# A two-layer token mixer in float32: the weight pairs of one chunk per MLP layer in another order

## The chip, the core and the metric

The kernel runs on one core of a Trainium2 chip. The metric is the device time of one execution in microseconds (us); the median of three runs of the kernel before is 2252.37 us (2251.97 to 2252.53). The engines are TensorE (PE, matrix products into the accumulator memory PSUM), VectorE (DVE) and ScalarE (ACT, both elementwise), GpSimd (POOL) and SyncE (SP, which here issues the loads). Each works through its own queue in order and waits at semaphores for the others.

## The reference

256 tokens of width 2048 go through two layers, in float32. Each layer is a mixer with an input and an output projection, and an MLP of hidden width 8192:

```python
for l in range(DEPTH):                                   # DEPTH = 2
    u = rmsnorm(h, g[0])
    ...                                                  # mixer: y
    h = h + rmsnorm(y, g[1])
    u = rmsnorm(h, g[2])
    z = jnp.square(jax.nn.relu(u @ mlp_w1[l])) @ mlp_w2[l]
    h = h + rmsnorm(z, g[3])
```

The change touches the product `u @ mlp_w1[l]` alone.

## The kernel before

**Split products.** Every float32 operand is split into a high part (a cast by ACT) and a residual (operand minus high part, by DVE). A product of two tiles is three matmuls into one accumulator: high x high, high x residual of the weight, residual of the activation x high. Lines 236 to 238 are these three in an ordinary block, lines 360 to 362 in the summed pairs described below.

**Tiling.** The 256 tokens are two row tiles (t = 0, 1) of 128. The width 2048 is sixteen k-tiles of 128. A load (L220, or L327 in the pairs) brings a slab: two k-tiles by 512 columns of a weight matrix, 512 KB, into one of seven `raw` tiles. ACT casts it to `whi` (L223, L331) and DVE forms `wlo` (L224, L332) in one of six pairs of tiles (`W_BUFS`). A slab of an ordinary block takes 12 matmuls.

**The MLP.** The hidden width is worked through in eight chunks of 1024 columns. For chunk c, `up(c)` computes the hidden values and `down(c)` multiplies them by 1024 rows of W2; the order is up(0), up(1), down(0), up(2), down(1) and so on. up(0) is two ordinary blocks of 512 columns. up(1) to up(7) are done by the class `Pairs`: eight pairs of k-tiles (k-tiles 2p and 2p + 1), each by the full 1024 columns, that is two slabs L (left 512 columns) and R. The string `PAIRS = "SSCSSCSC"` says how each pair is done.

- A **C** pair is ordinary: eight products of (row tile, column half, k-tile), 24 matmuls; two slabs, each cast once, two of the six tile pairs.
- An **S** pair is a 2 x 2 by 2 x 2 block product with seven products in place of eight, 21 matmuls. It needs sums of weight tiles and sums of activation tiles. The weight sums are four additions on DVE (L336), which overwrite the raw tiles; the pair then has `plain` (L as it is), `r1` (half of R), `two` (two sums) and `four` (two more sums), and takes four of the six tile pairs. The products are called p1, p2, q3, q5, p7, p6, q4; p1 and p2 use `plain`, q3 `r1`, q5 and p7 `two`, p6 and q4 `four`. The sums of activation tiles (class `Differences`, L294, L301, L304, L305) are made once per layer for the pairs 0, 1, 3, 4 and 6, during up(0).

Some products are shared by several outputs. After the last S pair (`end`), a copy on ACT (L392) and four additions on DVE (L373) combine them; the last C pair then finishes each output tile with another addition (L373) and the squared ReLU (L596). These are the twelve closing operations of DVE. The four output tiles are transposed by PE (L175, four matmuls each), split again (L162, L163), and are operands of down(1), one phase later. The hidden tiles of up(0) pass the same steps (L584, L586, L175, L162, L163) during the first pairs of up(1), and their transposes use the accumulators `acc` (three buffers), as do the products p1, p2 and bR; the other products use `aux` (five buffers).

**What sets the order.** `run` walks the slabs or pairs in order: load, then matmuls, then what is due (`later`, L422). A scheduler then orders each engine's queue ahead of the run; it may move a matmul or an addition past others that do not depend on it. On the chip the queues are fixed.

Of the kernel before, what the change touches and what calls it, by code (L numbers as in the profile page):

```python
# [22 lines left out]
NT = 2  # L23
# [2 lines left out]
W_BUFS = 6  # L26
LEAD = 6
PAIRS = "SSCSSCSC"
ACC_BUFS = 3
AUX_BUFS = 5  # L30
TAIL = 4
# [8 lines left out]
def trunk(ctx, tc, x, x_t, norm_g, ng_cols, e_win, rbf, e_wout, o_win, lbraw, smalls, wa2, ba, o_wout, w1, w2,  # L40
          c_ident, c_flip, c_mask, out):
    nc = tc.nc
# [7 lines left out]
    dram = ctx.enter_context(tc.tile_pool(name="dram", bufs=1, space=bass.MemoryType.DRAM))  # L50
    accp = ctx.enter_context(tc.tile_pool(name="accp", bufs=ACC_BUFS, space=PSUM))
    auxp = ctx.enter_context(tc.tile_pool(name="auxp", bufs=AUX_BUFS, space=PSUM))

    def aux():
        return auxp.tile([P, 512], F32, name="aux")
# [116 lines left out]
    def transpose4(src, pool=auxp, name="aux"):  # L172
        ps = pool.tile([P, 512], F32, name=name)
        for k in range(4):
            nc.tensor.transpose(out=ps[:, k * P:(k + 1) * P], in_=src[:, k * P:(k + 1) * P], identity=ident)  # L175
        return ps

    class XT:
        def __init__(self):
            self.g = {}  # L180
# [21 lines left out]
    def w_pair():  # L202
        return [wp.tile([P, SLAB, 512], F32R, name="w" + n) for n in ("hi", "lo")]

    class Block:
# [7 lines left out]
        def load(self, s):  # L213
            k0 = self.kts[s * SLAB]
            raw = rawp.tile([P, SLAB, 512], F32, name="raw")
            hi, lo = w_pair()
            n = slice(0, self.n)
            fine = s in self.fine
            for a, b in ((0, 1), (1, 2)) if fine else ((0, SLAB),):
                nc.sync.dma_start(out=raw[:, a:b, n], in_=self.wv[:, k0 + a:k0 + b, self.n0:self.n0 + self.n])  # L220
                if fine:
                    self.beside[a]()
                nc.scalar.copy(out=hi[:, a:b, n], in_=raw[:, a:b, n])  # L223
                nc.vector.tensor_tensor(out=lo[:, a:b, n], in0=raw[:, a:b, n], in1=hi[:, a:b, n], op=ALU.subtract)  # L224
            self.w[s] = (hi, lo)
# [84 lines left out]
    class Pairs:  # L310
# [6 lines left out]

        nslab = len(PAIRS)

        def __init__(self, wv, n0, X, diffs, U, evac):  # L320
            self.wv, self.n0, self.X, self.diffs, self.U, self.evac = wv, n0, X, diffs, U, evac
            self.w, self.ps = {}, {}

        def load(self, s):
            raws = [rawp.tile([P, SLAB, 512], F32, name="raw") for _ in range(2)]
            for raw, n in zip(raws, (self.n0, self.n0 + 512)):
                nc.sync.dma_start(out=raw, in_=self.wv[:, 2 * s:2 * s + 2, n:n + 512])  # L327

            def conv(raw, i=slice(0, SLAB)):
                hi, lo = w_pair()  # L330
                nc.scalar.copy(out=hi[:, i, :], in_=raw[:, i, :])  # L331
                nc.vector.tensor_tensor(out=lo[:, i, :], in0=raw[:, i, :], in1=hi[:, i, :], op=ALU.subtract)  # L332
                return hi, lo

            def add(dst, a, b):
                nc.vector.tensor_tensor(out=dst, in0=a, in1=b, op=ALU.add)  # L336

            L, R = raws
            if PAIRS[s] == "C":
                self.w[s] = [conv(L), conv(R)]  # L340
                return
            plain = conv(L)
            r1 = conv(R, slice(1, 2))
            add(R[:, 1, :], R[:, 1, :], R[:, 0, :])
            add(R[:, 0, :], R[:, 0, :], L[:, 0, :])
            two = conv(R)
            add(L[:, 0, :], L[:, 0, :], R[:, 1, :])
            add(L[:, 1, :], L[:, 1, :], L[:, 0, :])
            self.w[s] = [plain, r1, two, conv(L)]

        def product(self, n, s, x, w, i):
            first = n not in self.ps
            if first:
                self.ps[n] = accp.tile([P, 512], F32, name="acc") if n in ("bR", "p2", "p1") else aux()
            ps, (xh, xl), (hi, lo) = self.ps[n], x, w
            if n in ("q5", "p7", "p6", "p1"):
                stop = "S" not in PAIRS[s + 1:]
            else:
                stop = s == self.nslab - 1 and i == SLAB - 1
            nc.tensor.matmul(ps, xh, hi[:, i, :], start=first, stop=False)  # L360
            nc.tensor.matmul(ps, xh, lo[:, i, :], start=False, stop=False)  # L361
            nc.tensor.matmul(ps, xl, hi[:, i, :], start=False, stop=stop)  # L362

        def mm(self, s, t):
            if t == 0:
                return
            x = [[self.X.get(t, 2 * s + i) for i in range(2)] for t in range(NT)]
            w = self.w.pop(s)
            z = self.ps
            s1, u, u3 = self.U  # L370

            def add(n, a, b, op=ALU.add):
                nc.vector.tensor_tensor(out=n, in0=a, in1=b, op=op)  # L373

            if PAIRS[s] == "C":
                for n, t, j in (("p2", 0, 0), ("q3", 0, 1), ("q4", 1, 0), ("bR", 1, 1)):
                    for i in range(2):
                        self.product(n, s, x[t][i], w[j], i)
                    if s == self.nslab - 1:
                        o = self.out[t, j]  # L380
                        if j == 0:
                            add(o, z[n], s1 if t == 0 else u3)
                        else:
                            add(o, z[n], o)
                        self.evac(t, j, o)
                return
            d = self.diffs[s]
            L, r1, two, four = w
            end = "S" not in PAIRS[s + 1:]
            self.product("p1", s, x[0][0], L, 0)  # L390
            if end:
                nc.scalar.copy(out=s1, in_=z["p1"])  # L392
            self.product("p2", s, x[0][1], L, 1)
            self.product("q3", s, d.get(3), r1, 1)
            self.product("q5", s, d.get(0), two, 0)
            self.product("p7", s, d.get(2), two, 1)
            self.product("p6", s, d.get(1), four, 0)
            if end:
                self.out = {(t, j): self.evac.tile() for t in range(NT) for j in range(2)}
                add(u, z["p6"], s1)  # L400
                add(u3, z["p7"], u)
                add(self.out[0, 1], z["q5"], u, ALU.subtract)
                add(self.out[1, 1], z["q5"], u3, ALU.subtract)
            self.product("q4", s, x[1][1], four, 1)
# [17 lines left out]
    def later(f, slabs=2):  # L422

        soon.append([slabs, f])
# [50 lines left out]
    def wview(w):  # L475
        return w.rearrange("(kt p) n -> p kt n", p=P)
# [87 lines left out]
    def mlp(l, X, rst, factors, y, ypool, spool, mid, between, lead):  # L564
        diffs, U, late = {}, [], {}
        hid = {}
        w1v, w2v = wview(w1[l]), wview(w2[l])
# [12 lines left out]
        def up(c):  # L580
            def mk(j):
                def evac(t, ps):
                    r = ypool.tile([P, 512], F32, name="relu", bufs=2)
                    nc.scalar.activation(out=r, in_=ps, func=AF.Relu)  # L584
                    r2 = ypool.tile([P, 512], F32, name="ulo", bufs=4)
                    nc.vector.tensor_tensor(out=r2, in0=r, in1=r, op=ALU.mult)  # L586
                    later(lambda: hid[c].put(t, c * 2 + j, split4(x2p, "x2", transpose4(r2, accp, "acc"))))
                return evac

            hid[c] = Hid()  # L590
            if c == 0:
                return [Block(w1v, j * 512, 512, ALLK, X.get, mk(j)) for j in range(2)]
            n = [0]

            def evac(t, j, z):
                nc.vector.scalar_tensor_tensor(out=z, in0=z, scalar=0.0, in1=z, op0=ALU.max, op1=ALU.mult)  # L596
                n[0] += 1
                later(lambda: hid[c].put(t, c * 2 + j, split4(x2p, "x2", transpose4(z))), 2 + 2 * n[0])
            evac.tile = lambda: ypool.tile([P, 512], F32, name="ulo", bufs=4)
            return [Pairs(w1v, c * 1024, X, diffs, U, evac)]  # L600

        def down(c):
            def mk(nb):
# [19 lines left out]
        def difference(p):  # L623
            diffs[p] = Differences(spool, X, p)
            diffs[p].make(lambda: ypool.tile([P, 512], F32, name="relu", bufs=2))
# [5 lines left out]

        work = [lambda p=p: difference(p) for p in range(len(PAIRS)) if PAIRS[p] == "S"]
        hooks = {LEAD + 1 + 2 * i: [f] for i, f in enumerate(work)}
# [19 lines left out]
    X = XIn()  # L653
# [560 lines left out]
```

## Time and profile before

The table is taken from one profiled execution.

| | before |
|---|---|
| time of the profiled execution | 2252.14 us |
| its span, first to last instruction | 2250.3 us |
| median of three runs | 2252.37 us |
| mean granted TensorE clock | 0.999 |
| ACT busy | 1162.1 us (52%) |
| bytes moved | 440.87 MB, mean 196 GB/s |

The profile's timeline gives the start of an instruction, its duration, engine, line, operation, output and inputs, and in brackets how long the engine was idle before it and what ended that. A duration runs to the result's arrival: the next instruction of the same engine often starts before it. up(1) of layer 0 runs on PE from 431.97 to 474.93 us after the span's start; that of layer 1 is the same 1161.6 us later.

### The profile page before, as it was taken

How to read it: one execution, taken by the hardware profiler on the slowest of the kernel's cores; microseconds unless marked ns; L12 is line 12 of the kernel's file. 1: busy time of each engine (PE TensorE's matmuls, PEld its weight loads, DVE VectorE, ACT ScalarE, POOL GpSimd, SP SyncE). 2: the span in 40 equal slices, each digit the busy share in tenths (PEclk: the TensorE clock that was granted, in tenths of full speed). 3: DMA queues.
4: the chain of work that ended last, by engine and by line, in shares of the span. 5: the costliest groups of instructions: out<-in, count | busy, mean ns of one | idle time of the engine just before them, and what ended most of it. 6: DMA issues, size and time to landing. Idle time of an engine off the chain costs nothing.

```text
span 2250.3 us, 28788 instructions
## 1 busy us (share of the span) xinstructions
PE 2230.9 (99%) x10556; PEld 1849.3 (82%) x10556; DVE 1746.8 (78%) x2328; ACT 1162.1 (52%) x1598; POOL 20.6 (1%) x40
## 2 busy tenths in 40 slices
PE   9999999999999999999999999999999999999998
PEld 7888888888888888888788888888788888888886
DVE  6656656988898898896867767657979889889876
ACT  7444445655455455454746454546555445445443
POOL 0000000000000000000100000000000000000000
PEclk9999999999999999999999999999999999999999
DMA  9565576575565575586655545576556566566673
GB/s 348 167 181 169 169 265 187 175 231 171 187 230 167 187 237 158 197 288 192 212 174 166 152 150 156 170 241 201 156 196 233 160 206 218 169 207 202 198 262 101
DMA packets 222560, 440.87 MB, mean 196 GB/s; under 512 B 13745, under 2 KB 14545, under 8 KB 222417
## 3 DMA queue, kind: packets, MB, share of 16 engines
q1 hardware_dynamic: 218880, 429.18, 59.2%
q0 software_dynamic: 2816, 8.99, 1.1%
q8 instruction: 83, 1.36, 0.2%
q10 hardware_dynamic: 720, 0.85, 0.1%
q14 instruction: 61, 0.49, 0.1%
HBM read 430.57 MB, written 8.40 MB: 195 GB/s over the span
## 4 chain that ended last, share of the span: by engine, by line
PE 90%; DVE 6%; ACT 1%; issue 1%; DMA 1%; DVEq 0%; ACTq 0%; SPq 0%
PE acc L236 18%; PE acc L238 18%; PE acc L237 18%; PE aux L361 4%; PE aux L362 4%; PE aux L360 4%; PE acc L275 3%; PE aux L275 3%; PE acc L362 3%; PE acc L361 3%; PE acc L360 3%; PE aux L175 2%; DVE raw L336 2%; DVE wlo L332 2%; PE aux L272 2%; PE acc L272 2%
## 5 line engine op out<-in xcount | busy, mean ns | idle before, releaser
L224 DVE TENSOR_TENSOR wlo<-raw,whi 128x1024 fp32r<-128x1024 f32 (+1 forms) x561 | 676.2, 1220 | 343.4 <-ACT whi L223 341.5
L223 ACT CAST whi<-raw 128x1024 fp32r<-128x1024 f32 (+1 forms) x561 | 585.6, 1054 | 635.4 <-PE acc L238 486.1
L236 PE MATMUL acc<-whi,x 128*128 128x512 f32 x1280 | 502.9, 393 | 0.0
L331 ACT CAST whi<-raw 128x1024 fp32r<-128x1024 f32 x364 | 337.5, 968 | 319.4 <-DVE raw L336 214.0
L238 PE MATMUL acc<-whi,x 128*128 128x512 f32 x1280 | 498.9, 390 | 0.0
L237 PE MATMUL acc<-wlo,x 128*128 128x512 f32 x1280 | 498.7, 390 | 0.0
L332 DVE TENSOR_TENSOR wlo<-raw,whi 128x1024 fp32r<-128x1024 f32 x364 | 394.2, 1118 | 59.6 <-ACT whi L331 56.0
L238 PEld LDWEIGHTS acc<-whi,x 128*128 128x128 f32 x1280 | 240.3, 188 | 50.6
L237 PEld LDWEIGHTS acc<-wlo,x 128*128 128x128 f32 x1280 | 240.5, 188 | 48.5
L236 PEld LDWEIGHTS acc<-whi,x 128*128 128x128 f32 x1280 | 240.4, 188 | 48.4
L236 PE MATMUL acc<-whi,xt 128*128 128x512 f32 x640 | 253.5, 398 | 0.8 <-ACT xt L672 0.7
L237 PE MATMUL acc<-wlo,xt 128*128 128x512 f32 x640 | 250.8, 392 | 3.3 <-DVE wlo L224 2.1
L238 PE MATMUL acc<-whi,xt 128*128 128x512 f32 x640 | 250.5, 392 | 0.0
L336 DVE TENSOR_TENSOR raw<-raw 128x512 f32<-128x512 f32 x280 | 193.8, 692 | 9.3
L237 PEld LDWEIGHTS acc<-wlo,xt 128*128 128x128 f32 x640 | 120.3, 188 | 29.7 <-DVE wlo L224 6.3
L238 PEld LDWEIGHTS acc<-whi,xt 128*128 128x128 f32 x640 | 120.1, 188 | 25.9 <-DVE xt L168 0.6
L236 PEld LDWEIGHTS acc<-whi,xt 128*128 128x128 f32 x640 | 119.9, 188 | 25.9 <-ACT xt L672 1.6
L360 PE MATMUL acc<-whi,xt 128*128 128x512 f32 x308 | 120.1, 390 | 0.0
L362 PE MATMUL acc<-whi,xt 128*128 128x512 f32 x308 | 119.9, 389 | 0.0
L361 PE MATMUL acc<-wlo,xt 128*128 128x512 f32 x308 | 119.9, 389 | 0.0
L360 PE MATMUL aux<-whi,s 128*128 128x512 f32 x280 | 109.4, 392 | 2.3 <-ACT whi L331 2.3
L361 PE MATMUL aux<-wlo,s 128*128 128x512 f32 x280 | 110.5, 395 | 1.0 <-DVE wlo L332 1.0
(228 smaller groups left out, 2541.9 us busy)
## 6 DMA issues: line engine op xcount, KB each, us to landing
raw<-w SPq DMA_DIRECT2D x512, 512.0 KB, 4.9
raw<-o_win SPq DMA_DIRECT2D x112, 512.0 KB, 3.8
raw<-e_win SPq DMA_DIRECT2D x95, 512.0 KB, 3.9
raw<-e_wout SPq DMA_DIRECT2D x32, 512.0 KB, 4.1
raw<-o_wout SPq DMA_DIRECT2D x32, 512.0 KB, 4.0
s<-norm_g SPq DMA_DIRECT2D x8, 512.0 KB, 6.3
mid<-s POOLq DMA_DIRECT2D x8, 512.0 KB, 3.9
s<-mid SPq DMA_DIRECT2D x8, 512.0 KB, 7.1
```

The costliest lines, as they stand in the source:

```text
L223: nc.scalar.copy(out=hi[:, a:b, n], in_=raw[:, a:b, n])
L224: nc.vector.tensor_tensor(out=lo[:, a:b, n], in0=raw[:, a:b, n], in1=hi[:, a:b, n], op=ALU.subtract)
L236: nc.tensor.matmul(ps, xh, hi[:, i, 0:self.n], start=first, stop=False)
L237: nc.tensor.matmul(ps, xh, lo[:, i, 0:self.n], start=False, stop=False)
L238: nc.tensor.matmul(ps, xl, hi[:, i, 0:self.n], start=False, stop=last)
L275: nc.tensor.matmul(self.ps[j], hi[:, i, cs], x, start=s == 0 and i == 0, stop=False)
L331: nc.scalar.copy(out=hi[:, i, :], in_=raw[:, i, :])
L332: nc.vector.tensor_tensor(out=lo[:, i, :], in0=raw[:, i, :], in1=hi[:, i, :], op=ALU.subtract)
L336: nc.vector.tensor_tensor(out=dst, in0=a, in1=b, op=ALU.add)
L360: nc.tensor.matmul(ps, xh, hi[:, i, :], start=first, stop=False)
L361: nc.tensor.matmul(ps, xh, lo[:, i, :], start=False, stop=False)
L362: nc.tensor.matmul(ps, xl, hi[:, i, :], start=False, stop=stop)
```

## The change

For c = 1 alone, in both layers, the eight pairs are taken in the order START: pair 2 (a C), 0, 1, 5 (a C), 3, 4, 6, 7 (a C). The kinds in the order of work are C S S C S S S C, where they were S S C S S C S C. The other six chunks go through `range(8)` as before.

```diff
+START = (2, 0, 1, 5, 3, 4, 6, 7)
...
-        def __init__(self, wv, n0, X, diffs, U, evac):
+        def __init__(self, wv, n0, X, diffs, U, evac, seq):
...
+            self.seq = seq
+            self.kinds = "".join(PAIRS[p] for p in seq)
...
-                nc.sync.dma_start(out=raw, in_=self.wv[:, 2 * s:2 * s + 2, n:n + 512])
+                nc.sync.dma_start(out=raw, in_=self.wv[:, 2 * self.seq[s]:2 * self.seq[s] + 2, n:n + 512])
...
-            if PAIRS[s] == "C":
+            if self.kinds[s] == "C":
...
-                stop = "S" not in PAIRS[s + 1:]
+                stop = "S" not in self.kinds[s + 1:]
...
-            x = [[self.X.get(t, 2 * s + i) for i in range(2)] for t in range(NT)]
+            x = [[self.X.get(t, 2 * self.seq[s] + i) for i in range(2)] for t in range(NT)]
...
-            d = self.diffs[s]
+            d = self.diffs[self.seq[s]]
-            end = "S" not in PAIRS[s + 1:]
+            end = "S" not in self.kinds[s + 1:]
...
-            return [Pairs(w1v, c * 1024, X, diffs, U, evac)]
+            return [Pairs(w1v, c * 1024, X, diffs, U, evac, START if c == 1 else range(len(PAIRS)))]
```

Lines behind the new constant move down by one, lines behind the constructor by three: L332 becomes L335, L336 becomes L339, L373 becomes L376, L596 becomes L599, L586 becomes L589, L224 becomes L225, L236 to L238 become L237 to L239, L175 becomes L176. The number of instructions of each kind is the same. Three places of the queues follow, in layer 0; layer 1 is alike.

First, VectorE's queue at the first pairs. `wlo<-raw,whi` of 128x1024 is a residual of a whole slab, of 128x512 that of `r1`; `raw<-raw` are the additions of an S pair; `relu` and `s<-relu` belong to the activation sums, `ulo<-relu` to the hidden tiles of up(0). Before, from the third addition of the first S pair on:

```order
L336 TENSOR_TENSOR raw<-raw 128x512
L301 TENSOR_TENSOR relu<-relu 128x128
L336 TENSOR_TENSOR raw<-raw 128x512
L305 TENSOR_TENSOR s<-relu,s 128x512
L332 TENSOR_TENSOR wlo<-raw,whi 128x1024
L586 TENSOR_TENSOR ulo<-relu 128x512
L332 TENSOR_TENSOR wlo<-raw,whi 128x1024
L586 TENSOR_TENSOR ulo<-relu 128x512
L332 TENSOR_TENSOR wlo<-raw,whi 128x512
L336 TENSOR_TENSOR raw<-raw 128x512 x4
L332 TENSOR_TENSOR wlo<-raw,whi 128x1024
```

Of the change, from the residual of `two` of the first S pair (now the second pair) on, to the residuals behind the second S pair's additions:

```order
L335 TENSOR_TENSOR wlo<-raw,whi 128x1024
L589 TENSOR_TENSOR ulo<-relu 128x512 x2
L339 TENSOR_TENSOR raw<-raw 128x512
L335 TENSOR_TENSOR wlo<-raw,whi 128x1024 x2
L335 TENSOR_TENSOR wlo<-raw,whi 128x512
L164 TENSOR_TENSOR x_4028<-acc,x_4028 128x512
L339 TENSOR_TENSOR raw<-raw 128x512 x3
L164 TENSOR_TENSOR x_4036<-acc,x_4036 128x512
L335 TENSOR_TENSOR wlo<-raw,whi 128x1024
L339 TENSOR_TENSOR raw<-raw 128x512
L335 TENSOR_TENSOR wlo<-raw,whi 128x1024 x4
```

The fourth addition of an S pair stood ahead of another operation or among four in a row; in the first two S pairs it now stands alone, directly ahead of the residual of `four`, which is formed from the tile that it writes.

Second, VectorE's queue at the end of up(1), from the fourth additions of the last S pair on. `s<-aux`, `ulo<-aux` and `ulo<-acc` are the combinations, `ulo<-ulo` the squared ReLU. Before:

```order
L336 TENSOR_TENSOR raw<-raw 128x512 x4
L332 TENSOR_TENSOR wlo<-raw,whi 128x1024 x4
L373 TENSOR_TENSOR s<-aux,s 128x512
L224 TENSOR_TENSOR wlo<-raw,whi 128x1024
L373 TENSOR_TENSOR s<-aux,s 128x512
L373 TENSOR_TENSOR ulo<-aux,s 128x512 x2
L373 TENSOR_TENSOR ulo<-acc,s 128x512
L373 TENSOR_TENSOR ulo<-aux,ulo 128x512
L596 SCALAR_TENSOR_TENSOR ulo<-ulo 128x512 x2
L373 TENSOR_TENSOR ulo<-aux,s 128x512
L373 TENSOR_TENSOR ulo<-acc,ulo 128x512
L596 SCALAR_TENSOR_TENSOR ulo<-ulo 128x512 x2
```

Of the change:

```order
L335 TENSOR_TENSOR wlo<-raw,whi 128x1024 x3
L376 TENSOR_TENSOR s<-aux,s 128x512
L335 TENSOR_TENSOR wlo<-raw,whi 128x1024
L376 TENSOR_TENSOR s<-aux,s 128x512
L376 TENSOR_TENSOR ulo<-aux,s 128x512 x2
L376 TENSOR_TENSOR ulo<-acc,s 128x512
L376 TENSOR_TENSOR ulo<-aux,ulo 128x512
L599 SCALAR_TENSOR_TENSOR ulo<-ulo 128x512 x2
L376 TENSOR_TENSOR ulo<-aux,s 128x512
L376 TENSOR_TENSOR ulo<-acc,ulo 128x512
L599 SCALAR_TENSOR_TENSOR ulo<-ulo 128x512 x2
L225 TENSOR_TENSOR wlo<-raw,whi 128x1024 x3
```

The first residual of the next block (L224, now L225) stood second among the closing operations; now it stands behind all of them, and the residual of the last C pair's right slab has its place. On ScalarE the copy L392 stood directly ahead of the last C pair's casts; it now stands ahead of four casts, those of the last S pair's `two` and `four` and the last C pair's.

Third, TensorE's queue at the seam between up(1) and down(0), where `acc<-whi,x` and `acc<-wlo,x` are down(0)'s matmuls and `aux<-ident,ulo` the transposes of up(1)'s hidden tiles. Before, twelve matmuls of down(0) stand ahead of these rows (the last two of them shown), and two more transposes stand 93 matmuls behind them:

```order
L237 MATMUL acc<-wlo,x_3804 128x512
L238 MATMUL acc<-whi,x_3804 128x512
L236 MATMUL acc<-whi,x_3796 128x512
L236 MATMUL acc<-whi,x_3804 128x512
L175 MATMUL aux<-ident,ulo 128x128 x4
L236 MATMUL acc<-whi,x_3796 128x512
L175 MATMUL aux<-ident,ulo 128x128 x10
L237 MATMUL acc<-wlo,x_3796 128x512
```

Of the change, from the last matmul of up(1) on:

```order
L365 MATMUL acc<-whi,xt 128x512
L237 MATMUL acc<-whi,x_3796 128x512
L237 MATMUL acc<-whi,x_3804 128x512
L176 MATMUL aux<-ident,ulo 128x128 x8
L237 MATMUL acc<-whi,x_3796 128x512
L176 MATMUL aux<-ident,ulo 128x128 x8
L238 MATMUL acc<-wlo,x_3796 128x512
```

Three matmuls of down(0), all with a high part, now stand ahead of all sixteen transposes, where fifteen stood among fourteen.

More of the change, by code (lines that the diff above doesn't have):

```diff
@@ L373, in add @@
                 nc.vector.tensor_tensor(out=n, in0=a, in1=b, op=op)
-            if PAIRS[s] == "C":
+            if self.kinds[s] == "C":
                 for n, t, j in (("p2", 0, 0), ("q3", 0, 1), ("q4", 1, 0), ("bR", 1, 1)):
```

## The prediction

> **What bounds the kernel now.** I read the page first: part 1 for the engine that is full, part 4 for the chain that ends last, and then the waits of TensorE over the whole program.
>
> ```profile
> PE 2230.9 (99%) x10556; PEld 1849.3 (82%) x10556; DVE 1746.8 (78%) x2328; ACT 1162.1 (52%) x1598; POOL 20.6 (1%) x40
> PE 90%; DVE 6%; ACT 1%; issue 1%; DMA 1%; DVEq 0%; ACTq 0%; SPq 0%
> PE aux L360 <- ACT whi L331: 2.3, 4, 0.7
> ```
>
> TensorE (PE) is full, so time is lost or won only where PE has to wait. The largest wait of the program is four pauses of L360, the first matmul of a product in the summed pairs. The timeline of PE puts two of them into the first summed chunk of layer 0 and two into that of layer 1:
>
> ```profile
> 452.83 0.39 PE L360 MATMUL acc<-whi,xt 128*128 128x512 f32 x1
> 454.64 0.39 PE L362 MATMUL aux<-whi,s 128*128 128x512 f32 x1
> 455.44 0.73 PE L360 MATMUL aux<-whi,s 128*128 128x512 f32 x2 [0.40 <-ACT whi L331]
> 456.88 0.50 PE L360 MATMUL aux<-whi,s 128*128 128x512 f32 x1 [0.72 <-ACT whi L331]
> 459.29 0.39 PE L360 MATMUL acc<-whi,xt 128*128 128x512 f32 x1
> 474.93 0.39 PE L236 MATMUL acc<-whi,x 128*128 128x512 f32 x1
> 1617.06 0.73 PE L360 MATMUL aux<-whi,s 128*128 128x512 f32 x2 [0.42 <-ACT whi L331]
> 1618.51 0.51 PE L360 MATMUL aux<-whi,s 128*128 128x512 f32 x1 [0.72 <-ACT whi L331]
> ```
>
> From 459.29 to 474.93 stand a C, an S and a C pair, 24 + 21 + 24 = 69 matmuls, so one takes 15.64 / 69 = 0.2267 us. After the matmul at 454.64 the next one was due at 454.87 and came at 455.44 (0.57 lost); the two casts' matmuls there were done at 455.90 and the next came at 456.88 (0.98 lost). That is 1.55 us per layer, **3.1 us in all, which is the most that this change can win from that place**.
>
> What it waits for is VectorE (DVE). Its rows, the four additions L336 of each S pair as marks:
>
> ```profile
> 445.74 2.87 DVE L336 TENSOR_TENSOR raw<-raw 128x512 f32<-128x512 f32 x4
> 452.80 2.87 DVE L336 TENSOR_TENSOR raw<-raw 128x512 f32<-128x512 f32 x4
> 462.13 2.87 DVE L336 TENSOR_TENSOR raw<-raw 128x512 f32<-128x512 f32 x4
> 467.63 2.36 DVE L332 TENSOR_TENSOR wlo<-raw,whi 128x1024 fp32r<-128x1024 f32 x2 [0.20 <-ACT whi L331]
> 469.91 0.68 DVE L373 TENSOR_TENSOR s<-aux,s 128x512 f32<-128x512 f32 x1
> 478.23 2.36 DVE L224 TENSOR_TENSOR wlo<-raw,whi 128x1024 fp32r<-128x1024 f32 x2
> ```
>
> From mark to mark an S pair costs DVE 452.80 - 445.74 = 7.06 us, and S plus C 9.33, so C costs 2.27. PE needs 21 x 0.2267 = 4.76 for S and 5.44 for C. Five S and three C are 42.1 us of DVE against 40.1 of PE: in this chunk DVE is the slower engine, whatever the order, and only the lead it has at the start hides that. From 462.13 to 478.23 DVE shows one wait of 0.20. **The chunk is bound by the end of the DVE chain.**
>
> **The change, part by part.**
>
> ```profile
> raw<-w SPq DMA_DIRECT2D x512, 512.0 KB, 4.9
> 406.34 50.87 SPq L327 DMA_DIRECT2D raw<-w  x16
> 418.57 1.05 ACT L331 CAST whi<-raw 128x1024 fp32r<-128x1024 f32 x1 [1.70 <-PE acc L238]
> ```
>
> Loads: the same 16 transfers of 512 KB in the same places of SyncE's queue, from other rows of W1. I cost them at nothing: a transfer lands 4.9 us after its issue, and the first was issued 12.2 us ahead of its cast, so the seven raw tiles cover it; a transfer that came late would add its lateness to x below. Number and form of all matmuls, casts and DVE operations stay the same: no work is removed. What changes is where DVE has to wait, and how its queue meets PE's at the end.
>
> *Term 1, DVE's waits x in the first three pairs.* Ahead of the four additions of the third-last S (462.13 before) stand four S and two C in both orders, with the same differences, squares and splits between them. So this mark moves by just the DVE idle time that is added. The nearest rows:
>
> ```profile
> 420.51 1.22 DVE L332 TENSOR_TENSOR wlo<-raw,whi 128x1024 fp32r<-128x1024 f32 x1
> 422.25 0.69 DVE L294 TENSOR_TENSOR relu<-xt 128x512 f32<-128x512 f32 x1
> 422.85 0.69 DVE L332 TENSOR_TENSOR wlo<-raw,whi 128x512 fp32r<-128x512 f32 x1
> 423.45 0.69 DVE L301 TENSOR_TENSOR relu<-relu 128x128 f32<-128x128 f32 x3
> 424.06 0.69 DVE L336 TENSOR_TENSOR raw<-raw 128x512 f32<-128x512 f32 x1
> 429.28 0.68 DVE L336 TENSOR_TENSOR raw<-raw 128x512 f32<-128x512 f32 x1
> 430.04 0.69 DVE L305 TENSOR_TENSOR s<-relu,s 128x512 fp32r<-128x512 f32 x1
> 431.15 1.23 DVE L332 TENSOR_TENSOR wlo<-raw,whi 128x1024 fp32r<-128x1024 f32 x1 [0.42 <-ACT whi L331]
> 431.97 0.39 PE L360 MATMUL acc<-whi,xt 128*128 128x512 f32 x1
> ```
>
> A residual L332 needs the cast of the sum that the fourth addition has just made. Here this addition took its place of 0.60 us at 429.28, and the residual started at 431.15: 1.27 us later, of which an L305 filled 0.60. In the new queue (first listing of the change) the fourth addition of the first S and of the second S each stand directly ahead of their residual, with nothing between. So there are two full gaps of 1.27 where there was one with 0.67 left: 2.54 - 0.67 = 1.87.
>
> A third wait is new. There are six pairs of high and residual tiles. C takes two and the S behind it four, so all six are filled before PE is through C, and the next S must wait until PE has read C's left pair for the last time, its 18th matmul: 431.97 + 17 x 0.2267 + 0.39 = 436.21, plus the cast of 1.05 (418.57) gives 437.3. DVE comes there, from 420.51, after five full residuals of 1.13 (from the row at 467.63: two take 2.36, the second starting 1.13 after the first), twelve 512-wide operations of 0.60 (422.25 to 422.85), eight small ones of 0.20 (three from 423.45 to 424.06), three dependent additions 0.12 longer (four take 2.87 in the marks), and the gap of 1.27: 420.51 + 5.65 + 7.2 + 1.6 + 0.36 + 1.27 = 436.6. It waits 0.7. So x = 1.87 + 0.7 = 2.57. Its bounds: -0.67, if every cast comes ahead of DVE so that the old gap goes as well, and 3.4, if all three gaps come whole and no old one is credited (2.54 + 0.7, and 0.2 more for C's right pair). I take 2.57, what the nearest rows give, since the listing leaves DVE nothing else to do in the gaps.
>
> *Where PE stands.* Its fifth pair is now the first of three S in a row; it starts at 452.83 + 3 x 0.2267 = 453.5 (a C more, an S less ahead). DVE's marks for the three are 462.13 + 2.57 = 464.70 for the last, and 7.06 and 14.12 earlier: 450.6, 457.6, 464.7. In the trace PE's two-sum product came 455.44 - 452.80 = 2.64 after the mark, the next sum's 4.08 after it, and 2.27 (10 matmuls) later the pair was done. So the fifth pair doesn't wait; the sixth starts at 458.3, is at 11 matmuls at 460.8 and waits to 457.6 + 4.08 = 461.7 (0.9), ending at 464.0; the seventh waits to 467.3 (1.3) and to 468.8 (1.0), ending at 471.0; C ends at 476.5. The old stall of 1.55 is gone, and 3.2 come in its place: PE reaches the next block 1.6 us late.
>
> *Term 2, the seam to the next block.* This decides, since DVE is later still.
>
> ```profile
> 466.07 0.57 ACT L392 COPY s<-acc 128x512 f32<-128x512 f32 x1
> 466.55 2.00 ACT L331 CAST whi<-raw 128x1024 fp32r<-128x1024 f32 x2
> 478.11 0.60 PE L175 MATMUL aux<-ident,ulo 128*128 128x128 f32 x4
> 478.47 0.48 PE L236 MATMUL acc<-whi,x 128*128 128x512 f32 x1
> 478.79 1.25 PE L175 MATMUL aux<-ident,ulo 128*128 128x128 f32 x10
> 479.80 0.47 PE L237 MATMUL acc<-wlo,x 128*128 128x512 f32 x1
> ```
>
> Before, the residual of the next block's first slab (L224) was the second operation behind 469.91, ahead of the rest of the twelve closing operations, and PE had 15 matmuls of this block and 14 transposes (0.09 each: four from 478.11 to 478.47) to do up to 479.80, without a wait. In the new queue a residual of the last C has that place, and the block's first residual comes behind all twelve. DVE's end of them: 478.23 less the one L224 ahead of it (1.13), so 477.1, less the wait of 0.20 at 467.63, whose cause, the copy of 466.07 on ScalarE ahead of the last C's casts, now stands ahead of the last S's casts too, plus x: 479.5. Then the residual, 1.23 long: 480.7. Up to it PE has 3 matmuls and 16 transposes, 2.1 us behind 476.5, and so waits some 2 us. Compared at equal work: 480.7 - 479.8 = 0.9, plus 12 matmuls still to do (2.72), less two transposes (0.18): 3.44 us later.
>
> *Sum:* the shift of a layer is 0.87 + x. 2 x 3.44 = **6.9 us**. The profiled execution took 2252.14, so 2259.0; the median of the runs is 0.23 above it: **2259.3**. Behind the seam the block has slack (C-like slabs, one residual of 1.13 per 12 matmuls of 2.72), so nothing grows there, and it gives nothing back to a full PE. The first product of the second pair now waits for an accumulator that two transposes use; its place is now the end of that pair, and a wait there up to a DVE split (0.60) hides under DVE's lateness of some 2 us at the seam.
>
> **The clock gate.** The windows view (length, busy PE, then the other engines, granted clock, DMA share, GB/s; the first row PE alone) at the old pause and at the program's end, and PE's timeline at its opening:
>
> ```profile
> 452.83:459.29 6.46, 5.34 (x22) 1.00 0.42 133
> 2240.00:2250.00 10.00, 1.48 (x7) 0.90 (x5) 6.48 (x14) 1.31 (x4) 0.00 (x0) 0.74 0.57 211
> 1.22 4.45 PE L682 MATMUL aux<-warm 128*128 128x512 bf16 x10 [1.22 <-DVE uT L871]
> ```
>
> Pauses of 0.57 and 0.98 left the granted clock at 1.00; the last ten microseconds, with 1.48 of PE work, show 0.74; the ten opening matmuls took 4.45 us where ten take 2.27 later. At the new seam PE has 3 matmuls in 4.2 us, with transposes and waits between. If that counts as idle, some ten matmuls of each layer go at the opening's pace: 2 x 2.2 = 4.4 us more. [...]
>
> **Rivals.** (1) *DVE keeps its pace*: x is about 0, since casts run ahead. Then a layer loses only 0.87 at the seam: 2252.4 + 1.7 = 2254.1, within 0.2% (4.5 us, about what a measurement of this kernel can tell from no change). For it: from 445.74 on DVE hardly waits. Against: the listing. The point between the cases is x = 1.4. (2) *Not slower*: beginning with C gives PE 5.44 us of work for 2.27 of DVE, the lead outlasts the three S, the seam is covered, and the 3.1 us are won: 2249.3, within 0.2%. The place is the DVE chain from 420.51 to the first residual of the next block; it decides from x = -0.87 on, so DVE would have to finish almost 1 us earlier than before. Against: no DVE work is taken away. (3) *The clock falls at the seam*: 2259.3 + 4.4 = 2263.7.
>
> **Chances.** Forecast 0.76, (1) 0.12, (2) 0.05, (3) 0.06; 0.01 is left. The bounds of x give 2 x 0.2 = 0.4, so 2252.8, and, with x = 3.4 and the 0.2 kept, 2 x 4.5 = 9.0, so 2261.4. Range 2252.7 to 2261.5. Slower by over 0.2%: the forecast but for its lowest part, and (3): 0.80. Within: 0.18. Faster: 0.02.
>
> **What would show it.** Right: in each layer DVE waits over 1 us twice for a cast near 434 and 444; the last four additions near 464.7; PE without a wait in the fifth pair, about 1, 1.3 and 1 us in the sixth and seventh; the old 455.44 pause gone; some 2 us of PE waits for DVE around the transposes, the first residual matmul near 480.7 (and 1161.6 later in layer 1); granted clock 1.00. Wrong: a last mark near 462, PE through the three S without a pause, or no wait at the transposes.

## The result and the profile after

The changed kernel takes **2259.31 us** (median of 7 runs, 2258.53 to 2260.16) against 2252.37 (7 runs, 2251.97 to 2252.81): a ratio of 1.0031, 95% interval 1.0022 to 1.0041. It is slower by 6.9 us. The span of the profiled execution is 2257.1 us, 6.8 more than before, and its time is 2258.88.

From the page of the changed kernel, the span and part 1, and from its waits of TensorE the two that grew and one that is new:

```profile
span 2257.1 us, 28797 instructions
PE 2233.0 (99%) x10556; PEld 1849.7 (82%) x10556; DVE 1746.7 (77%) x2328; ACT 1163.1 (52%) x1598; POOL 20.6 (1%) x40
```

```profile
PE aux L363 <- ACT whi L334: 4.8, 6, 1.0
PE acc L238 <- DVE wlo L225: 3.1, 6, 0.6
PE acc L237 <- DVE ulo L376: 0.5, 2, 0.3
```

The busy time of every engine is what it was within 2.1 us (DVE 1746.7 against 1746.8, PE 2233.0 against 2230.9). No work was added: time went into waits. L363, the old L360, waits 4.8 us in six pauses in place of 2.3 in four. The second row stood at this before:

```profile
PE acc L237 <- DVE wlo L224: 2.1, 4, 0.6
```

Its two more waits, and the two of the third row, are those at the seams to the next block, one of each kind per layer.

VectorE at the first pairs, timeline of the changed kernel:

```profile
433.72 0.68 DVE L339 TENSOR_TENSOR raw<-raw 128x512 f32<-128x512 f32 x1
435.52 1.23 DVE L335 TENSOR_TENSOR wlo<-raw,whi 128x1024 fp32r<-128x1024 f32 x1 [1.12 <-ACT whi L334]
437.33 1.83 DVE L335 TENSOR_TENSOR wlo<-raw,whi 128x1024 fp32r<-128x1024 f32 x2 [0.58 <-ACT whi L334]
...
443.46 0.69 DVE L339 TENSOR_TENSOR raw<-raw 128x512 f32<-128x512 f32 x1
445.35 5.24 DVE L335 TENSOR_TENSOR wlo<-raw,whi 128x1024 fp32r<-128x1024 f32 x5 [1.20 <-ACT whi L334]
...
457.69 2.87 DVE L339 TENSOR_TENSOR raw<-raw 128x512 f32<-128x512 f32 x4
464.75 2.87 DVE L339 TENSOR_TENSOR raw<-raw 128x512 f32<-128x512 f32 x4
```

Three waits stand where one of 0.42 stood, 1.12 + 0.58 + 1.20 = 2.90. The mark that stood at 462.13 stands at 464.75, 2.62 later. The middle wait is named as one for a cast; ScalarE's row shows what that cast had waited for:

```profile
436.24 1.06 ACT L334 CAST whi<-raw 128x1024 fp32r<-128x1024 f32 x1 [0.75 <-PE aux L365]
```

It was a matmul of PE (L365), which had to be through with the pair of tiles that the cast overwrites.

PE's pauses and the seam, timeline of the changed kernel:

```profile
461.77 0.50 PE L363 MATMUL aux<-whi,s 128*128 128x512 f32 x1 [0.72 <-ACT whi L334]
467.36 0.73 PE L363 MATMUL aux<-whi,s 128*128 128x512 f32 x2 [0.98 <-ACT whi L334]
468.81 0.50 PE L363 MATMUL aux<-whi,s 128*128 128x512 f32 x1 [0.72 <-ACT whi L334]
...
476.69 0.62 PE L237 MATMUL acc<-whi,x 128*128 128x512 f32 x2
477.15 1.03 PE L176 MATMUL aux<-ident,ulo 128*128 128x128 f32 x8
478.42 0.47 PE L237 MATMUL acc<-whi,x 128*128 128x512 f32 x1 [0.24 <-DVE ulo L376]
478.93 1.26 PE L176 MATMUL aux<-ident,ulo 128*128 128x128 f32 x8
480.66 0.50 PE L238 MATMUL acc<-wlo,x 128*128 128x512 f32 x1 [0.48 <-DVE wlo L225]
```

PE reaches the next block at 476.69 and has three matmuls and sixteen transposes up to 480.66. By the prediction's count these are about 2.1 us of work (3 x 0.2267 + 16 x 0.09) in 3.97; the brackets show only part of the rest as idle, since a duration runs on past the start of the next matmul (a row of one matmul shows 0.39 us where they come 0.2267 apart). Two of the three matmuls stand ahead of the transposes, the third between their two groups of eight. What it waits for is the first residual L225, behind the last closing operations. VectorE there, and PE's stretch in the windows view (columns as in the prediction, PE, weight loads, DVE, ACT, POOL, then the granted clock):

```profile
478.19 1.29 DVE L599 SCALAR_TENSOR_TENSOR ulo<-ulo 128x512 f32<-128x512 f32 x2
479.39 3.49 DVE L225 TENSOR_TENSOR wlo<-raw,whi 128x1024 fp32r<-128x1024 f32 x3
```

```profile
476.69:480.66 3.97, 3.22 (x20) 2.15 (x18) 3.97 (x7) 3.12 (x6) 0.00 (x0) 1.00 0.18 70
```

VectorE is busy for the whole of it, and the granted clock is 1.00.

### The profile page after: what moved, and what is told of

The parts are those of the page before. It is cut to its first block, busy times and chain, and to the rows that moved or that the text cites. A ratio compares the mean times of both kernels' runs of the same rounds, so it can differ in the third digit from the quotient of the medians.

```text
span 2257.1 us, 28797 instructions
## 1 busy us (share of the span) xinstructions
PE 2233.0 (99%) x10556; PEld 1849.7 (82%) x10556; DVE 1746.7 (77%) x2328; ACT 1163.1 (52%) x1598; POOL 20.6 (1%) x40
## 4 chain that ended last, share of the span: by engine, by line
PE 90%; DVE 6%; ACT 1%; issue 1%; DMA 1%; DVEq 0%; ACTq 0%; SPq 0%
PE acc L239 19%; PE acc L238 19%; PE acc L237 19%; PE aux L364 4%; PE aux L365 4%; PE aux L363 4%; PE acc L276 3%; PE aux L276 3%; PE acc L363 2%; PE acc L365 2%; PE acc L364 2%; DVE raw L339 2%; PE aux L176 2%; DVE wlo L335 2%; PE aux L273 2%; PE acc L273 2%
## 5 line engine op out<-in xcount | busy, mean ns | idle before, releaser
L225 DVE TENSOR_TENSOR wlo<-raw,whi 128x1024 fp32r<-128x1024 f32 (+1 forms) x561 | 675.9, 1220 | 346.1 <-ACT whi L224 343.5
L224 ACT CAST whi<-raw 128x1024 fp32r<-128x1024 f32 (+1 forms) x561 | 585.5, 1053 | 638.3 <-PE acc L239 487.7
L237 PE MATMUL acc<-whi,x 128*128 128x512 f32 x1280 | 502.9, 393 | 0.5 <-DVE ulo L376 0.5
L238 PE MATMUL acc<-wlo,x 128*128 128x512 f32 x1280 | 498.9, 390 | 1.0 <-DVE wlo L225 1.0
L239 PE MATMUL acc<-whi,x 128*128 128x512 f32 x1280 | 499.0, 390 | 0.0
L335 DVE TENSOR_TENSOR wlo<-raw,whi 128x1024 fp32r<-128x1024 f32 x364 | 394.2, 1118 | 64.3 <-ACT whi L334 60.5
L238 PEld LDWEIGHTS acc<-wlo,x 128*128 128x128 f32 x1280 | 240.5, 188 | 50.2 <-DVE wlo L225 1.4
L239 PEld LDWEIGHTS acc<-whi,x 128*128 128x128 f32 x1280 | 240.3, 188 | 50.4
L237 PEld LDWEIGHTS acc<-whi,x 128*128 128x128 f32 x1280 | 240.4, 188 | 49.2 <-ACT whi L224 0.5
L237 PE MATMUL acc<-whi,xt 128*128 128x512 f32 x640 | 253.6, 398 | 1.2 <-ACT xt L675 1.2
L238 PE MATMUL acc<-wlo,xt 128*128 128x512 f32 x640 | 250.9, 392 | 3.4 <-DVE wlo L225 2.2
L239 PE MATMUL acc<-whi,xt 128*128 128x512 f32 x640 | 250.5, 392 | 0.0
L339 DVE TENSOR_TENSOR raw<-raw 128x512 f32<-128x512 f32 x280 | 193.8, 692 | 9.2
L238 PEld LDWEIGHTS acc<-wlo,xt 128*128 128x128 f32 x640 | 120.3, 188 | 29.6 <-DVE wlo L225 4.7
L239 PEld LDWEIGHTS acc<-whi,xt 128*128 128x128 f32 x640 | 120.2, 188 | 25.8 <-DVE xt L169 0.6
L237 PEld LDWEIGHTS acc<-whi,xt 128*128 128x128 f32 x640 | 119.9, 188 | 26.1 <-ACT xt L675 1.7
L363 PE MATMUL acc<-whi,xt 128*128 128x512 f32 x308 | 120.4, 391 | 0.0
L365 PE MATMUL acc<-whi,xt 128*128 128x512 f32 x308 | 120.0, 390 | 0.0
L363 PE MATMUL aux<-whi,s 128*128 128x512 f32 x280 | 109.5, 393 | 4.8 <-ACT whi L334 4.8
```

The costliest lines, as they stand in the source:

```text
L237: nc.tensor.matmul(ps, xh, hi[:, i, 0:self.n], start=first, stop=False)
L238: nc.tensor.matmul(ps, xh, lo[:, i, 0:self.n], start=False, stop=False)
L239: nc.tensor.matmul(ps, xl, hi[:, i, 0:self.n], start=False, stop=last)
```

## The experiments

The theory was that a layer loses 0.87 us at the seam plus the added waits x of VectorE, and that both go through one chain, the DVE queue of the chunk. The main rivals were that three S pairs in a row near the end are the cause (they drain PE), and that PE's own pauses add up. Runs of the kernel before on the same chips gave 2252.39 us (first four experiments), 2252.40 (next three) and 2252.27 (last two).

**e1: the three S pairs early.** The order still begins with the C, but the run of three S follows it at once (C SSS C SS C).

```diff
-START = (2, 0, 1, 5, 3, 4, 6, 7)
+START = (2, 0, 1, 3, 5, 4, 6, 7)
```

> Order C S S S C S S C in place of C S S C S S S C; same kinds, same first pair, same last two. VectorE's chain theory: ahead of the last S stands the same work with the same three waits (about 1.1, 0.6 and 1.2 us near 435.5, 437.3 and 445.3), so the last mark of four additions stays near 464.7 and the first residual of the next block near 479.4; TensorE's pauses move (two of about 0.9 near 451 and smaller ones near 467) but the seam is reached at the same time: 2259.3, no more than 0.7 from the changed kernel. Rival, that three S pairs standing last in a row are what starves TensorE: with only two S ahead of the last C the last pauses go back to the 1.55 us of before, and with them about 1.6 us of each layer: 2256.1.

2259.02 us (2258.68 to 2259.65), ratio 1.0030 [1.0018, 1.0043]. PE's pauses are others, four in place of three, and VectorE's end is the same to 0.01 us:

```profile
450.99 0.73 PE L363 MATMUL aux<-whi,s 128*128 128x512 f32 x2 [0.72 <-ACT whi L334]
452.44 0.50 PE L363 MATMUL aux<-whi,s 128*128 128x512 f32 x1 [0.72 <-ACT whi L334]
467.50 0.73 PE L363 MATMUL aux<-whi,s 128*128 128x512 f32 x2 [0.26 <-ACT whi L334]
468.81 0.50 PE L363 MATMUL aux<-whi,s 128*128 128x512 f32 x1 [0.58 <-ACT whi L334]
```

```profile
464.75 2.87 DVE L339 TENSOR_TENSOR raw<-raw 128x512 f32<-128x512 f32 x4
...
479.40 3.48 DVE L225 TENSOR_TENSOR wlo<-raw,whi 128x1024 fp32r<-128x1024 f32 x3
```

Where the three S stand does not matter: the last mark and the first residual of the next block are where they were, and these are VectorE's. The first rival falls. The second stays open here, since PE's idle times in the chunk are nearly as long in sum as those of the changed kernel (2.28 us against 2.42); e4 decides it.

**e2: without the C at the beginning.** The kinds are SS CC SSS C: the seam of the changed kernel (its closing order, PE's three matmuls among the transposes) with the beginning of the kernel before.

```diff
-START = (2, 0, 1, 5, 3, 4, 6, 7)
+START = (0, 1, 2, 5, 3, 4, 6, 7)
```

> Order S S C C S S S C: it begins with S as before, but keeps the three S in a row ahead of the last C and the closing queue of the changed kernel. VectorE's chain theory: without a C in front x is about 0 (only the old wait of 0.42 near 431.2), so the last mark is near 462.1 and only the seam is lost, about 0.9 to 1.1 us a layer: 2254.1 to 2254.7. Rival, three S in a row: they are still there, so the loss stays: 2259.3. Rival, that the seam alone makes the loss: 2259.3 as well.

2254.73 us (2254.38 to 2255.06), ratio 1.0010 [1.0002, 1.0019]. From its DVE timeline:

```profile
431.16 1.23 DVE L335 TENSOR_TENSOR wlo<-raw,whi 128x1024 fp32r<-128x1024 f32 x1 [0.42 <-ACT whi L334]
...
462.39 2.87 DVE L339 TENSOR_TENSOR raw<-raw 128x512 f32<-128x512 f32 x4
...
477.03 3.48 DVE L225 TENSOR_TENSOR wlo<-raw,whi 128x1024 fp32r<-128x1024 f32 x3
```

The old wait of 0.42 is back, the three waits are gone, and the mark is near its old place. From mark to L225 it is 14.64 us here, in e1 (14.65) and in the changed kernel (464.75 to 479.39, 14.64). So what the beginning with a C costs reaches the seam undiminished: the marks are 464.75 - 462.39 = 2.36 apart, and 2 x 2.36 = 4.7 is the difference of the times, 2259.31 - 2254.73 = 4.6 us. The other 2254.73 - 2252.39 = 2.3 come with the new end, 2 x 0.26 of it from a mark that is 0.26 later than before.

**e3: the gaps filled.** The order of the change, but both additions of `four` are issued ahead of the cast and residual of `two`, so that the residual of `two` fills the gap behind the fourth addition.

```diff
             add(R[:, 0, :], R[:, 0, :], L[:, 0, :])
-            two = conv(R)
             add(L[:, 0, :], L[:, 0, :], R[:, 1, :])
             add(L[:, 1, :], L[:, 1, :], L[:, 0, :])
+            two = conv(R)
```

> The changed kernel, with the four additions of an S pair written ahead of the casts of its sums, so that the residual of the first two sums stands between the fourth addition and the residual of the last two. VectorE's chain theory: both gaps of 1.1 to 1.2 us behind the fourth addition go. The first one's gain is eaten by the wait for a pair of tiles that ends at 437.3 whatever VectorE does (0.58 grows to about 1.7); the second one's stays: the last mark moves from 464.75 to about 463.6, 1.15 us a layer, 2256.9 to 2257.1. If the wait for the pair of tiles were not fixed by TensorE, both gaps would be won: 2254.7. Rival, that these gaps lie under TensorE's work and three S in a row set the time: 2259.3.

2256.80 us (2256.54 to 2258.27), ratio 1.0020 [1.0011, 1.0029]; 2.5 us won. Its profile's times lie 0.45 later than those of the changed kernel from the chunk's first matmul on (432.41 against 431.96). From its DVE timeline:

```profile
434.76 1.22 DVE L335 TENSOR_TENSOR wlo<-raw,whi 128x1024 fp32r<-128x1024 f32 x1
437.78 1.83 DVE L335 TENSOR_TENSOR wlo<-raw,whi 128x1024 fp32r<-128x1024 f32 x2 [1.80 <-ACT whi L334]
...
442.77 0.68 DVE L339 TENSOR_TENSOR raw<-raw 128x512 f32<-128x512 f32 x1
443.37 4.78 DVE L335 TENSOR_TENSOR wlo<-raw,whi 128x1024 fp32r<-128x1024 f32 x4
...
464.06 2.87 DVE L339 TENSOR_TENSOR raw<-raw 128x512 f32<-128x512 f32 x4
```

Both gaps are gone, but the wait for a pair of tiles has grown from 0.58 to 1.80 and ends at 437.78 - 0.45 = 437.33, where it ended in the changed kernel (437.33). Its end belongs to PE: the cast ahead of it waits for L365 here too and starts at 436.69 - 0.45 = 436.24, as it did there. So filling the first gap won nothing, and the whole gain is that of the second: 2 x 1.20 = 2.4 of the 2.5 us.

**e4 and e9: the residual ahead of the closing operations.** The order of the change; the load, cast and residual of down(0)'s first slab are issued ahead of the last C's products, so that L225 no longer stands behind all twelve closing operations: in the queue that results it stands behind four of them. PE's queue follows: 14 matmuls of down(0) stand ahead of the first transpose, where two stood. e9 is the same kernel again.

```diff
-            run(up(c))
+            downs = down(c - 1)
+            if c == 1:
+                first, plain = downs[0], downs[0].load
+                first.load = lambda s: plain(s) if s else None
+                run(up(c), hooks={7: [lambda: plain(0)]})
+            else:
+                run(up(c))
...
-            run(down(c - 1), hooks=hooks)
+            run(downs, hooks=hooks)
```

> The changed kernel, with the load of the next block's first slab issued ahead of the last C pair's products, so that its residual stands ahead of the closing operations as it did before the change. VectorE's chain theory with the seam: TensorE can do the twelve matmuls of that slab while VectorE closes; the marks stay (last at 464.75), the pauses of 1.0, 1.3 and 1.0 us stay, but the waits around the transposes (about 2 us) shrink to about 0.5: about 1.5 us a layer, 2256.2. Rival, that the seam only shows a lateness that TensorE has from its own pauses: 2259.3.

2257.10 us (2255.70 to 2257.48), ratio 1.0019 [1.0010, 1.0028]. PE has no wait at the seam any more, while its pauses in the chunk are the same as in the changed kernel. So these pauses by themselves don't set the time (the second rival falls), and the seam's place is right; but the time is 0.9 above what I expected. The profile shows why: a fall of the granted clock behind the pauses. First two stretches of the windows view, with the last two pauses and behind them, then PE's timeline.

```profile
466.10:469.50 3.40, 1.70 (x6) 0.80 (x6) 3.30 (x5) 2.44 (x3) 0.00 (x0) 1.00 0.19 73
469.50:473.00 3.50, 3.50 (x10) 2.68 (x9) 2.32 (x3) 3.50 (x5) 0.00 (x0) 0.51 0.61 187
```

```profile
467.75 0.73 PE L363 MATMUL aux<-whi,s 128*128 128x512 f32 x2 [0.97 <-ACT whi L334]
469.20 0.50 PE L363 MATMUL aux<-whi,s 128*128 128x512 f32 x1 [0.72 <-ACT whi L334]
469.54 0.58 PE L364 MATMUL aux<-wlo,s 128*128 128x512 f32 x1
469.92 0.63 PE L365 MATMUL aux<-whi,s 128*128 128x512 f32 x1
470.35 0.63 PE L364 MATMUL aux<-wlo,s 128*128 128x512 f32 x1
```

From 469.5 to 472.9 the matmuls are 0.43 us apart in place of 0.227, eight of them, which is 8 x 0.2 = 1.6 us lost. VectorE's first closing operation then waited 1.18 us for PE:

```profile
472.72 0.69 DVE L376 TENSOR_TENSOR s<-aux,s 128x512 f32<-128x512 f32 x1 [1.18 <-PE aux L365]
...
476.26 1.21 DVE L225 TENSOR_TENSOR wlo<-raw,whi 128x1024 fp32r<-128x1024 f32 x1
```

The eleven times lie in two groups, five from 2255.70 to 2256.09 and six from 2257.10 to 2257.48, and the profiled one (2257.41) is of the upper.

> e4_residual_ahead once more, unaltered (the first residual of the next block ahead of the closing operations). [...] Theory B (the fall follows from the order of the instructions): every profile shows it at the same place, whatever its time, and the two groups have another cause.

2255.98 us (2255.69 to 2257.64), ratio 1.0018 [1.0009, 1.0027]: eight times from 2255.69 to 2256.09 and three from 2257.33 to 2257.64. This profile (2255.98) is of the lower group. The same two stretches, and PE's timeline there:

```profile
466.10:469.50 3.40, 1.69 (x7) 0.80 (x6) 3.30 (x5) 2.42 (x3) 0.00 (x0) 1.00 0.29 109
469.50:473.00 3.50, 3.50 (x16) 2.84 (x16) 3.50 (x4) 3.50 (x5) 0.00 (x0) 1.00 0.66 201
```

```profile
467.77 0.73 PE L363 MATMUL aux<-whi,s 128*128 128x512 f32 x2 [0.98 <-ACT whi L334]
469.23 0.50 PE L363 MATMUL aux<-whi,s 128*128 128x512 f32 x1 [0.72 <-ACT whi L334]
469.56 0.40 PE L364 MATMUL aux<-wlo,s 128*128 128x512 f32 x1
469.80 0.40 PE L365 MATMUL aux<-whi,s 128*128 128x512 f32 x1
```

The pauses are the same to 0.01 us, the busy time ahead is the same (1.69 and 1.70), and so is the order, but the clock holds at 1.00 (VectorE's first closing operation starts at 471.48, without a wait). So the instructions alone don't set the fall: one profiled execution has it, the other has not. The medians of the two groups of all 22 runs, 2255.88 and 2257.38, are 1.5 us apart, and the mean granted clock is 0.998 in all nine of the upper group and 0.999 in all thirteen of the lower; from this, and from the 1.6 us lost in e4's profile, I estimate that a fall costs 1.5 us. Without it the residual alone wins 2259.31 - 2255.88 = 3.4 us, where 2259.3 - 2256.2 = 3.1 was expected. If some executions behind the 2259.31 hold falls too (see e8), it is a little less: the spans of the profiles without a fall, 2257.1 and 2257.6 against 2254.2, give 2.9 to 3.4.

**e5: both mended**, e3 and e4 together.

> The changed kernel with both mends, the four additions ahead of the casts and the next block's first residual ahead of the closing operations. If the two are separate terms, their gains add: 2.5 us for the first and 2.2 us for the second, as measured one by one, so 2254.6. If they are one and the same lateness seen twice, the second adds little: 2256.5. VectorE's chain still waits about 1.8 us for a pair of tiles near 437.3, which neither mend touches, so the time of before is not reached.

2253.56 us (2253.37 to 2254.64), ratio 1.0006 [0.9997, 1.0015]. The gain is 5.75, and the time is 1.0 better than expected. The sum that I had expected was made with e4's median, which is of the upper group; with e4's lower group it is 2.5 + 3.4 = 5.9. So the two parts add, as they should if one chain sets the end.

**e6: four C pairs.** The chunk's kinds are SSCCSCSC, in the order of k-tiles of the kernel before; one S has become a C, without weight sums and with 24 matmuls in place of 21.

```diff
+EASY = "SSCCSCSC"
...
-            self.kinds = "".join(PAIRS[p] for p in seq)
+            self.kinds = kinds or "".join(PAIRS[p] for p in seq)
...
-            return [Pairs(w1v, c * 1024, X, diffs, U, evac, START if c == 1 else range(len(PAIRS)))]
+            return [Pairs(w1v, c * 1024, X, diffs, U, evac, range(len(PAIRS)), EASY if c == 1 else PAIRS)]
```

> The order of before in all chunks, but in the first summed chunk of each layer one S pair (the fourth) is done as an ordinary one: S S C C S C S C. TensorE has three more matmuls a layer (0.68 us), VectorE 7.06 - 2.27 = 4.8 us less. VectorE's chain theory: VectorE needs 37.3 us against TensorE's 40.8, so the old pause of 1.55 us goes and nothing is late at the seam: 2 x (0.68 - 1.55) = -1.7, at most -2.3 with the small waits at the seam: 2250.1 to 2250.7. Rival, that the pause comes from two S in a row whatever VectorE's total: no two S stand in a row behind the first two, so the same. Rival, that the lead is lost in the first two pairs: the pause stays and 1.4 us are added: 2253.8.

2250.91 us (2250.71 to 2251.54), ratio 0.9993 [0.9985, 1.0002]. The interval still holds 1, but all 11 times lie below all 27 of the kernel before (2252.05 to 2253.07). PE has no pause left in the chunk, in either layer. The time is 0.2 above the upper end of what I expected. It is the fastest of the versions: 1.5 us below the kernel before, with three matmuls more per layer.

**e7: e2 with e4's residual.** No C at the beginning, and the residual ahead of the closing operations.

> Order S S C C S S S C with the next block's first residual ahead of the closing operations. Both terms of the loss are out, the three S in a row are kept. VectorE's chain theory with the seam: x is about 0.25 (last mark at 462.4 as measured without the mend), one pause of 0.9 us in place of 1.55, and no loss at the seam: 2251.5 to 2252.4, not slower than before. Rival, that the seam's loss comes from three S in a row: 2254.7, as without the mend.

2251.28 us (2251.05 to 2251.82), ratio 0.9995 [0.9986, 1.0004]. That is 0.2 below the range that I expected. The interval holds 1, but here too all 11 times lie below all 27 of the kernel before. Against e2 the seam's loss of 2.3 us is gone, and 3.45 are won in all, much as e4 won 3.4. The pause that is left is one of 0.69 us idle per layer, where the kernel before shows 0.40 and 0.72. So three S in a row can be had without a loss, if the next block's first residual is moved as well; by the order of the pairs alone (e2) 2.3 us are lost. The change's 6.9 us are thus the 4.6 of the beginning with a C (e2) and the 3.4 of the place of L225, less the 1.1 that this version wins.

**e8: the changed kernel again**, to see whether its clock falls too.

> The changed kernel itself, unaltered, in more executions. Theory A (the clock can fall after the pauses): e4_residual_ahead showed a granted clock of 0.51 from 469.5 to 473.0 and its eleven times lie in two groups, 2255.70 to 2256.09 and 2257.10 to 2257.48. The changed kernel has the same three pauses (0.72, 0.98, 0.72), so its times, 2258.53 to 2260.16 so far, should also fall into two groups 1.2 to 1.6 us apart, some near 2258.8 and some near 2260.1; a profile taken from the upper group shows a stretch of 3 to 4 us with a granted clock near 0.5 right after the pauses of a layer, one from the lower group none. Theory B (the fall belongs to the order of e4_residual_ahead alone): one group, with a spread of about that of before (0.9 us), and a granted clock of 1.00 in any profile.

2259.65 us (2258.90 to 2260.99, 5 runs), ratio 1.0033 [1.0021, 1.0046]. This is inconclusive: the twelve times of the two rounds lie between 2258.53 and 2260.99 without a clear gap. Both profiles, of 2258.88 and of 2259.41 us, show a granted clock of 1.00 in this stretch. All five times from 2259.83 up have a mean granted clock of 0.998, and of the seven up to 2259.65 one has, the others 0.999; that fits falls in the slower executions, but no profile of this kernel shows one, and the mean alone doesn't tell: the profile of 2258.88 has 0.998 with no fall ahead of the program's last microseconds (1.00 up to 2250.0, 0.56 from there to 2253.0). e1 is a control of a kind: its PE is idle for less at one place (0.72 and 0.72, then 0.26 and 0.58), and its six times lie within 0.97 us, all with 0.999, where those of the changed kernel spread over 2.46.

| version | us, median | against before |
|---|---|---|
| changed | 2259.31 | +6.9 |
| changed again, e8 | 2259.65 | +7.4 |
| e1, three S early | 2259.02 | +6.6 |
| e4 / e9, residual ahead | 2257.10 / 2255.98 | +4.7 / +3.7 |
| e3, gaps filled | 2256.80 | +4.4 |
| e2, no C first | 2254.73 | +2.3 |
| e5, e3 and e4 | 2253.56 | +1.2 |
| e7, e2 and e4 | 2251.28 | -1.1 |
| e6, four C | 2250.91 | -1.5 |

## Why the prediction was right

**Term 1, VectorE's waits.** Predicted x = 2.57 and a last mark at 464.70; the mark came at 464.75. The two gaps, foretold at 1.27 each, are 435.52 - 434.32 = 1.20 and 445.35 - 444.06 = 1.29 from the end of the addition's place of 0.60 us; the wait for a pair of tiles was 0.58 (0.7 foretold) and ended at 437.33 (437.3). What the prediction did not see is that its three waits are not independent. e3 shows that the first gap lies under the wait for tiles: with that gap gone the wait ends at the same moment. The sum isn't hurt by it, for it takes the wait as what the first gap leaves up to 437.3; the bounds are. The lower bound of x, -0.67, and with it rival (1), which asks for casts ahead of VectorE, were too kind: in e3, where no cast of a sum is waited for, the mark still moved by 464.06 - 0.45 - 462.13 = 1.5. That is the part that belongs to six pairs of tiles. Taking away that wait by itself (a seventh pair) changes the memory of the whole program and was not tried. One slip: the prediction calls the S of the mark at 462.13 the third-last; it is the last, and it is for the last that four S and two C stand ahead in both orders.

**PE's pauses.** Predicted: none in the fifth pair, 0.9 up to 461.7, then 1.3 up to 467.3 and 1.0 up to 468.8, C's end at 476.5. They ended at 461.77, 467.36 and 468.81, and the block at 476.69. e1 shows that they could have stood elsewhere at the same price: behind them PE is still ahead of VectorE.

**Term 2, the seam.** Predicted: twelve closing operations ahead of L225, first residual matmul at 480.7. It came at 480.66. At equal work this is 480.66 - 479.80 + 2.72 - 0.18 = 3.40 us (3.44 foretold), and layer 1 is alike; 2 x 3.40 = 6.8 is the difference of the spans. Of e2's 2.3 us, the 2 x 0.26 of its later mark belong to term 1; the 1.8 that are left are the seam by itself, where 2 x 0.87 = 1.7 was foretold. e4 and e9 show that the place in the queue is the cause: with the residual ahead of eight of the closing operations, and PE's matmuls of its slab with it ahead of the transposes, PE waits nowhere at the seam.

**The number.** That the median is 2259.31 where 2259.3 was forecast is in part luck. The runs spread over 1.6 us, some of the slower ones may hold a fall of the clock, which is no term of the sum, and the profiled execution without one took 2258.88. What bears the forecast out is the 3.40 us of each layer and where they are lost.

**Edits costed at nothing.** No pause of PE in the chunk ends at a load, and the wait foretold to be hidden at the end of the second pair does not show in the time: e2, which has no such order at its beginning, and the changed kernel differ by what their marks differ.

**Rivals.** (1) needed x below 1.4, and x was 2.6; e3 is the nearest to it, 1.5. (2) held that the C at the beginning gives VectorE a lead; e2, without that C, is 4.6 us faster than the change. What would have made the order no slower is shown by e7: the old beginning and another place for L225. (3) was wrong in its place and right in its kind. At the seam the granted clock is 1.00. But in e4's profile it is 0.51 from 469.5 to 473.0, behind the three pauses and not at the transposes. No run shows the 2 x 2.2 = 4.4 us that the rival added; by the two groups of e4 and e9 a fall costs 1.5 us, an estimate. The prediction weighed the pauses by those of the kernel before (0.57 and 0.98, granted clock 1.00) and let them pass.

## What to carry to other kernels

When an engine that is not full (here VectorE at 77% of the span) is the slower one in one stretch, price a new order by its queue there, up to the first instruction that the next stretch needs: a wait that the order put into that queue reached the seam whole here (2.36 us a layer). Beginning with a block that takes the full engine long filled the ring of buffers early here and made the helper wait for it (0.58 us, and 1.80 once it came sooner), which used up its lead. Issue the first operand of the next stretch ahead of this one's closing operations; here that was worth 3.4 of the 6.9 us.

## What the runs showed of the hardware that was not expected

The granted clock of TensorE was 0.51 from 469.5 to 473.0 in e4's profile, with 1.00 from 466.0 to 469.5 and from 473.0 to 480.0, although PE's longest idle time ahead of it in the chunk was 0.97 us. In the 3.40 us before it (466.10 to 469.50) PE was busy for 1.70, with two pauses, of 0.97 and 0.72 idle. The same queue, with the same pauses to 0.01 us and PE busy for 1.69, kept 1.00 in e9's profile, and 9 of the 22 runs lie in the slower group. In both profiles of the changed kernel PE is busy for 1.69 us from 466.10 to 469.50 too, and the granted clock stays at 1.00 from 469.5 to 473.0. So neither the pauses nor PE's busy time in this stretch tells the execution with the fall from the three without; what decides was not shown. In e1's profile PE is busy for 2.66 of 3.50 us (466.0 to 469.5), the granted clock is 1.00 behind it, and the six times lie within 0.97 us; in e6, which has no pause in the chunk, the eleven times lie within 0.83 us.

The other surprise is a quiet one: sixteen transposes with three matmuls and 1.9 us of waits, at the seam of the changed kernel (476.69 to 480.66), left the granted clock at 1.00 there and from 480.66 to 484.10. What rival (3) supposed of such a seam did not show.
